# A decoder layer's output product by Strassen's scheme: seven products of half blocks in place of eight

## The chip, the cores and the metric

The kernel runs on one core of one Trainium2 chip. The metric is the device time of one execution in microseconds (us). All times here are of one core. A core has TensorE (PE in the profile; its weight loads have a row of their own, PEld), VectorE (DVE), ScalarE (ACT), GpSimd (POOL) and SyncE (SP, which issues most DMAs). They work at the same time; each takes its own instructions in a fixed order.

## The reference

One layer of a hybrid decoder, on 512 tokens of width 1024, in float32:

```python
h = rms_norm(x, norm_g[l])
proj = h @ w_in[l]
hq, hf, hi, hz, cq, ckv, kr, mz, glog = jnp.split(proj, pts, axis=-1)
y_a = hgrn2_branch(hq, hf, hi, hz, lower_bounds[l], hg_norm_g[l])
y_b = mla_branch(cq, ckv, kr, mz, q_a_g[l], w_uq[l], kv_a_g[l], w_ukv[l])
gates = jax.nn.sigmoid((glog + b_gate[l]).astype(jnp.float32)) ...
merged = gates[:, :, 0] * (y_a @ w_proj_a[l]) + gates[:, :, 1] * (y_b @ w_proj_b[l])
x = x + merged @ w_out[l]
return rms_norm(x, final_norm_g)
```

The change concerns only `merged @ w_out`, a product of 512x1024 with 1024x1024, and what stands right around it: the addition to x and the last RMSNorm.

## The kernel before

Every float32 product is made of three matmuls on a faster format (`mm3`, lines 87 to 92): each operand is split into a high half, rounded to that format, and a low half, the rest; high x high, high x low and low x high are summed in PSUM. The split (`split`, lines 151 to 154) is a copy on ScalarE, which makes the high half, and a subtraction on VectorE, which makes the low half. Weights are loaded by SP's DMAs into a raw tile (pool `wraw`, three buffers) and split into tiles `w_hi` and `w_lo` (pools `whi` and `wlo`, four buffers each; line 111 the copy, 112 the subtraction).

The stage ahead of the change merges the two branches (lines 760 to 791). For each of four groups of 256 channels, and each branch, it makes the gates' logits (a product with the tiles hT, which hold the normed input) and a projection, and combines them. In the second branch VectorE forms (tanh + 1) * projection (line 786), GpSimd adds it into `ma`, the merged activations (line 787), and `split` writes the two halves of `ma` to `m` (line 788). Activations lie with channels on the partitions: `ma[:, j]` holds 128 channels of 512 tokens.

The output stage follows (lines 794 to 842). A block of `w_out` is 128 rows (one k of eight) by all 1024 columns: `load_wo` loads it through `wraw` and splits it into tiles named `wo`. For k from 0 to 3 the weights arrive one by one, and for each k all four blocks of 128 tokens and both halves of the columns are multiplied, into eight PSUM accumulators. Then k from 4 to 7 are finished token block by token block. Behind each half row stand: an addition of half the accumulator to x (line 830, VectorE, out of PSUM; `merged` carries a factor of 2), the sum of squares (833, ScalarE), a product with the norm's gain `fg` (834, VectorE), small operations for the norm on GpSimd (835, 836), the scaling by ScalarE (839) and VectorE (841), and two output DMAs (840 on ScalarE's queue, 842 on SP's).

The program is written with a tile framework: it places waits between instructions that share a tile, and orders the instructions of an engine by a planner, which follows the order of the program as far as its own estimate of readiness allows. Where no `manual_schedule` block stands (none does in the output stage), the order on an engine is the planner's. Pools opened on the same side lie behind each other in memory and take over the memory of closed ones; a tile in such memory waits for the last reader of the tile that lay there. The pool `w_out` on the left thus follows `hpool`, with the tiles hT, whose last readers are the gates' products of the last group of the second branch.

Of the kernel before, what the change touches and what calls it, by code (L numbers as in the profile page):

```python
# [18 lines left out]
P = 128  # L19
D = 1024  # L20
S = 512
NT = S // P
KD = D // P
# [6 lines left out]
EPS = 1e-6  # L30
# [3 lines left out]
N_MM = 3  # L34
WCH = 1024
# [3 lines left out]
def hybrid_layer(ctx: ExitStack, tc: tile.TileContext, a):  # L39
    nc = tc.nc  # L40
# [46 lines left out]
    def mm3(ps, l, r, lsl, rsl, start, stop):  # L87

        (lh, ll), (rh, rl) = l, r
        nc.tensor.matmul(ps, lh[lsl], rh[rsl], start=start, stop=False)  # L90
        nc.tensor.matmul(ps, lh[lsl], rl[rsl], start=False, stop=False)  # L91
        nc.tensor.matmul(ps, ll[lsl], rh[rsl], start=False, stop=stop)  # L92
# [58 lines left out]
    def split(hi, lo, src):  # L151

        last_split[0] = nc.scalar.copy(hi, src)  # L153
        nc.vector.tensor_tensor(lo, src, hi.bitcast(F32), op=ALU.subtract)  # L154
# [17 lines left out]
    neg_half, eps = fixed[:, 0:4], fixed[:, 4:5]  # L172
# [46 lines left out]
    half = [slice(n * 512, n * 512 + 512) for n in range(2)]  # L219
# [54 lines left out]
    with tc.manual_schedule(engines={mybir.EngineType.PE, mybir.EngineType.Activation, mybir.EngineType.DVE}):  # L274
# [17 lines left out]
        sq, rs = st.tile([P, D], F32, "sq", bufs=2), rss[0]  # L292
        v, y, e = [st.tile([P, 1], F32, f"rsq{i}") for i in range(3)]
# [32 lines left out]
        lo = [turned(1, 0), turned(1, 1)]  # L326
        for t in range(1, NT):
# [14 lines left out]
            lo = nxt  # L342
# [5 lines left out]
    ps = ax_tile()  # L348
# [33 lines left out]
    for t in range(NT):  # L382
        ps = mm_tile()
# [22 lines left out]
    for j in range(5):  # L406
        ps = ax_tile()
        for t in range(NT):
# [3 lines left out]
                                       op0=ALU.mult, op1=ALU.subtract)  # L412
    ps = ax_tile()
# [319 lines left out]
    for h in range(H):  # L733
# [12 lines left out]
        if h % 4 == 0:  # L746
            v = mla_values(h)
# [12 lines left out]
    def merge(b, c, y, wp, g=None):  # L760
        return list(zip(g or gates(b, c), proj_ch(wp, c * 256, y)))
# [9 lines left out]
    ma = mp.tile([P, KD, S], F32, "ma")  # L771
# [5 lines left out]
            nc.vector.scalar_tensor_tensor(ma[:, 2 * c + i], g[:], 1.0, ps[:], op0=ALU.add, op1=ALU.mult)  # L777
    yap.close()
    m2p = Pool("merged_parts", "right")
    m = [m2p.tile([P, KD, S], F32R, f"m{i}") for i in range(2)]  # L780
    ybsp = Pool("yb_parts", "right")
    ybs = parts(ybsp, yb, "yb")
    for c in range(4):
        for i, (g, ps) in enumerate(merge(1, c, ybs, a["w_proj_b"][0])):
            j = 2 * c + i
            nc.vector.scalar_tensor_tensor(g[:], g[:], 1.0, ps[:], op0=ALU.add, op1=ALU.mult)  # L786
            nc.gpsimd.tensor_tensor(ma[:, j], ma[:, j], g[:], op=ALU.add)  # L787
# [10 lines left out]
    acc = [mm_tile() for _ in range(N_MM)] + [ax_tile() for _ in range(8 - N_MM)]  # L798
    acc = [acc[2 * t : 2 * t + 2] for t in range(NT)]
    wo = a["w_out"][0].rearrange("(k p) c -> p k c", p=P)  # L800

    def load_wo(k):
        raw = wraw.tile([P, WCH], F32, tag="raw", name="wo_raw")
        hl = [wop.tile([P, 1, D], F32R, f"wo{i}", 4) for i in range(2)]
        nc.sync.dma_start(raw[:], wo[:, k, :])
        split(hl[0][:, 0], hl[1][:, 0], raw[:])
        return hl

    def out_mm(k, t, o, n, w):
        mm3(acc[t][o // 512][:, o % 512 : o % 512 + n], m, w, (slice(None), k, slice(t * P, t * P + P)),  # L810
            (slice(None), 0, slice(o, o + n)), k == 0, k == KD - 1)

    for k in range(4):
        w = load_wo(k)
        for t in range(NT):
            for o in (0, 512):
                out_mm(k, t, o, 512, w)
    ws = [load_wo(k) for k in range(4, KD)]
    nc.sync.dma_start(fg[:], a["final_norm_g"].partition_broadcast(P))
    for t in range(NT):  # L820
        nc.sync.dma_start(xr[t][:], a["x"][0, t * P : t * P + P, :])
    for t in range(NT):
        last = t == NT - 1
        ss = op.tile([P, 3], F32, "ss", bufs=2)
        rg = op.tile([P, D], F32, "rg", bufs=2)
        for i, (o, n) in enumerate(((0, 512), (512, 512))):
            sl = slice(o, o + n)
            for k in range(4, KD):
                out_mm(k, t, o, n, ws[k - 4])
            nc.vector.scalar_tensor_tensor(xr[t][:, sl], acc[t][o // 512][:, o % 512 : o % 512 + n], 0.5, xr[t][:, sl],  # L830
                                           op0=ALU.mult, op1=ALU.add)
            sq = op.tile([P, 512], F32, "sq", bufs=2)
            nc.scalar.activation(sq[:, :n], xr[t][:, sl], AF.Square, accum_out=ss[:, i : i + 1])
            nc.vector.tensor_tensor(rg[:, sl], xr[t][:, sl], fg[:, sl], op=ALU.mult)
            nc.gpsimd.tensor_scalar(ss[:, 0:1], ss[:, i : i + 1], 1.0 / D, ss[:, 0:1] if i else EPS, op0=ALU.mult, op1=ALU.add)
        nc.gpsimd.tensor_tensor(ss[:, 0:1], ss[:, 0:1], neg_half[:, 0:1], op=ALU.pow)
        o = a["out"][0, t * P : t * P + P, :]
        c = 384 if last else 512
        nc.scalar.activation(rg[:, :c], rg[:, :c], AF.Copy, scale=ss[:, 0:1])
        nc.scalar.dma_start(o[:, :c], rg[:, :c])  # L840
        nc.vector.tensor_scalar(rg[:, c:], rg[:, c:], ss[:, 0:1], None, op0=ALU.mult)
        nc.sync.dma_start(o[:, c:], rg[:, c:])
    wop.close()
    op.close()
    m2p.close()
    mp.close()
    edge.close()
# [38 lines left out]
```

## Time and profile before

| | before |
|---|---|
| median of 3 runs | 633.08 us (632.96 to 633.23) |
| the profiled execution's own time | 633.0 us |
| its span, first to last instruction | 631.2 us |
| mean granted TensorE clock | 0.998 |
| busy, ScalarE | 239.6 us (38%) |
| first and last matmul of the output stage start | 580.7 and 624.0 us |

How to read the rows shown in the prediction. On the profile's page, an engine has its busy time, the share of the span, and its number of instructions; the chain that ended last is followed back from the last instruction, and its shares tell which engine's work set the time. A row of a tile gives the line of the kernel, the engine, the operation, output<-inputs, the count, the shortest, median and longest duration in ns, and the first and last start in us. A row of the timeline gives the start, the duration in us, the engine, the line and the operation, with the tile's form, and in brackets how long the engine had been idle and what ended that. A row of the table by stretches gives the busy time of PE, PEld, DVE, ACT and POOL, each with its number of instructions, then the granted clock as a share of full speed, the DMA share, and GB/s. A row of the chain has start, duration, engine and line. A row of DMA issues has the queue, the number, the size of each and the median us from issue to landing.

### The profile page before, as it was taken

Reading aid. Unit: us, or ns where it says so; the run is one execution under the profiler, and the core shown is the slowest. Engines: PE = TensorE matmul, PEld = TensorE weight load, DVE = VectorE, ACT = ScalarE, POOL = GpSimd, SP = SyncE. Lnnn points to the kernel's source line nnn. Section 1 sums busy time; section 2 is a strip of 40 time slices with the busy share of each in tenths; the row PEclk is TensorE's granted clock in tenths of the full one; section 3 lists DMA queues with packets and bytes.
Section 4 is the critical chain, followed back from the end, with each engine's and each line's share of the span. In section 5 each row is a group of like instructions: output and inputs, shape, how many; then the busy total and the mean of one; then the engine's idle time right before and its main releaser. Section 6 shows DMA issues by size and latency. Waiting matters only on the chain.

```text
span 631.2 us, 8391 instructions
## 1 busy us (share of the span) xinstructions
PE 621.8 (99%) x3204; PEld 523.4 (83%) x3204; DVE 353.5 (56%) x552; ACT 239.6 (38%) x451; POOL 115.1 (18%) x213
## 2 busy tenths in 40 slices
PE   8999999999999999999999999999999999999995
PEld 5998888888888888888888888888888888888884
DVE  7727855397855459757566756583322342434244
ACT  5554242323233232355445645382222222323223
POOL 3106300332310033331213141000000010111011
PEclk9999999999999999999999999999999999999999
DMA  8325153124114203322332243213333323325403
GB/s 271 121 63 182 47 167 86 48 67 125 43 38 137 74 21 88 93 62 73 84 96 72 55 130 91 78 37 101 100 101 100 101 73 113 101 82 159 174 16 118
DMA packets 58809, 59.75 MB, mean 95 GB/s; under 512 B 5737, under 2 KB 52239, under 8 KB 58769
## 3 DMA queue, kind: packets, MB, share of 16 engines
q1 hardware_dynamic: 56636, 55.60, 29.5%
q10 hardware_dynamic: 1988, 3.09, 1.7%
q8 instruction: 25, 0.41, 0.3%
q0 software_dynamic: 144, 0.52, 0.3%
q14 instruction: 16, 0.12, 0.1%
HBM read 55.01 MB, written 2.10 MB: 90 GB/s over the span
## 4 chain that ended last, share of the span: by engine, by line
PE 93%; DVE 2%; ACT 2%; POOL 1%; issue 1%; DMA 0%; ACTq 0%; POOLq 0%
PE mm_ps L90 25%; PE mm_ps L92 25%; PE mm_ps L91 25%; PE ax_ps L92 2%; PE ax_ps L91 2%; PE ax_ps L90 2%; PE mm_ps L264 1%; PE ax_ps L664 1%; PE ax_ps L685 1%; PE ax_ps L508 1%; PE ax_ps L229 1%; PE ax_ps L527 1%; PE ax_ps L529 1%; PE ax_ps L496 1%; PE ax_ps L516 1%
## 5 line engine op out<-in xcount | busy, mean ns | idle before, releaser
L112 DVE TENSOR_TENSOR w_lo<-w_raw,w_hi 128x1024 fp32r<-128x1024 f32 (+3 forms) x90 | 109.1, 1216 | 131.5 <-ACT w_hi L111 130.2
L111 ACT CAST w_hi<-w_raw 128x1024 fp32r<-128x1024 f32 (+3 forms) x90 | 89.3, 995 | 179.4 <-PE mm_ps L91 130.0
L90 PE MATMUL mm_ps<-hT,w_hi 128*128 128x512 f32 x384 | 150.8, 393 | 0.0
L91 PE MATMUL mm_ps<-hT,w_hi 128*128 128x512 f32 x384 | 149.8, 390 | 0.0
L92 PE MATMUL mm_ps<-hT,w_lo 128*128 128x512 f32 x384 | 149.6, 391 | 0.0
L92 PEld LDWEIGHTS mm_ps<-hT,w_lo 128*128 128x128 f32 x384 | 72.1, 188 | 14.9
L91 PEld LDWEIGHTS mm_ps<-hT,w_hi 128*128 128x128 f32 x384 | 72.2, 188 | 14.4
L90 PEld LDWEIGHTS mm_ps<-hT,w_hi 128*128 128x128 f32 x384 | 72.2, 188 | 14.2
L787 POOL TENSOR_TENSOR ma<-ma,z 128x512 f32<-128x512 f32 x8 | 11.8, 1479 | 176.9 <-DVE z L786 176.9
L91 PE MATMUL mm_ps<-w_lo,hT 128*128 128x512 f32 (+1 forms) x96 | 36.5, 382 | 0.0
L92 PE MATMUL mm_ps<-w_hi,hT 128*128 128x512 f32 (+1 forms) x96 | 36.4, 382 | 0.0
L90 PE MATMUL mm_ps<-w_hi,hT 128*128 128x512 f32 (+1 forms) x96 | 36.4, 386 | 0.0
L672 POOL TENSOR_SCALAR p<-p,sm 128x128 f32<-128x128 f32 (+3 forms) x28 | 16.9, 606 | 72.9 <-DVE sm L669 59.5
L453 DVE RECIPROCAL tf<-pr 128x512 f32<-128x512 f32 x8 | 26.8, 3349 | 0.2
L670 ACT ACTIVATE p<-ax_ps,sm 128x128 f32<-128x128 f32 (+3 forms) x32 | 16.9, 529 | 25.0 <-DVE sm L669 24.9
L91 PE MATMUL mm_ps<-ya,w_hi 128*128 128x512 f32 x64 | 25.0, 390 | 0.0
L92 PE MATMUL mm_ps<-ya,w_lo 128*128 128x512 f32 x64 | 24.9, 389 | 0.0
L90 PE MATMUL mm_ps<-yb,w_hi 128*128 128x512 f32 x64 | 24.9, 389 | 0.0
L91 PE MATMUL mm_ps<-yb,w_hi 128*128 128x512 f32 x64 | 24.9, 389 | 0.0
L92 PE MATMUL mm_ps<-yb,w_lo 128*128 128x512 f32 x64 | 24.9, 389 | 0.0
L90 PE MATMUL mm_ps<-ya,w_hi 128*128 128x512 f32 x64 | 24.8, 389 | 0.0
L154 DVE TENSOR_TENSOR wo<-wo_raw,wo 128x1024 fp32r<-128x1024 f32 x8 | 9.6, 1223 | 25.9 <-ACT wo L153 25.9
(226 smaller groups left out, 1123.8 us busy)
## 6 DMA issues: line engine op xcount, KB each, us to landing
w_raw<-w_in SPq DMA_DIRECT2D x58, 512.0 KB, 3.8
w_raw<-w_proj_a SPq DMA_DIRECT2D x8, 512.0 KB, 3.4
w_raw<-w_proj_b SPq DMA_DIRECT2D x8, 512.0 KB, 3.4
wo_raw<-w_out SPq DMA_DIRECT2D x8, 512.0 KB, 3.9
xr<-x SPq DMA_DIRECT2D x4, 512.0 KB, 8.9
w_raw<-w_in SPq DMA_DIRECT2D x4, 448.0 KB, 5.0
x<-x SPq DMA_DIRECT2D x3, 512.0 KB, 7.2
w_raw<-w_uq SPq DMA_DIRECT2D x8, 192.0 KB, 2.7
```

The costliest lines, as they stand in the source:

```text
L90: nc.tensor.matmul(ps, lh[lsl], rh[rsl], start=start, stop=False)
L91: nc.tensor.matmul(ps, lh[lsl], rl[rsl], start=False, stop=False)
L92: nc.tensor.matmul(ps, ll[lsl], rh[rsl], start=False, stop=stop)
L111: nc.scalar.copy(hi[:, :o], raw[:, :o])
L112: (lo_eng or nc.vector).tensor_tensor(lo[:, :o], raw[:, :o], hi[:, :o].bitcast(F32), op=ALU.subtract)
L154: nc.vector.tensor_tensor(lo, src, hi.bitcast(F32), op=ALU.subtract)
L229: nc.tensor.matmul(idle[:], zero[:, :P], zero[:], start=True, stop=True)
L264: nc.tensor.matmul(ps, hT[l][:, 4 * kh + k, t * P : t * P + P], c_hl[kh][r][:, k * 256 : k * 256 + 256], start=kh == 0 and kind == 0 and k ...
L453: nc.vector.reciprocal(rp[:], pr[:])
L670: nc.scalar.activation(p[:, :n], sps[:, :n], AF.Exp, scale=SCALE, bias=sm[:, 1:2], accum_out=sm[:, 2:3])
L672: (nc.vector if final else nc.gpsimd).tensor_scalar(p[:, :n], p[:, :n], sm[:, 3:4], 0.5, op0=ALU.mult, op1=ALU.mult)
L787: nc.gpsimd.tensor_tensor(ma[:, j], ma[:, j], g[:], op=ALU.add)
```

## The change

The token-by-k matrix is cut into four blocks: A11 (tokens 0 to 255, channels 0 to 511), A12 (the same tokens, channels 512 to 1023), A21 and A22 (tokens 256 to 511); `w_out` into B11, B12, B21, B22 of 512 x 512. The four blocks of the output are made of seven products of blocks by the scheme of Strassen in Winograd's form, in place of eight. In the order of the code, with the name that the diff gives each operand:

| | product | operand of activations | operand of weights | goes to |
|---|---|---|---|---|
| P1 | A11 B11 | m_top | w11 | u, and output 11 |
| P2 | A12 B21 | m_bot, first tokens | w21 | output 11 |
| P3 | S1 T1 | s1 = A21 + A22 | t1 = B12 - B11 | outputs 22 and 12 |
| P4 | S2 T2 | s2 = S1 - A11 | t2 = B22 - T1 | u, output 12 |
| P5 | A22 T4 | m_bot, last tokens | t4 = B21 - T2 | output 21 |
| P6 | S3 T3 | s3 = A11 - A21 | t3 = B22 - B12 | u, outputs 21 and 22 |
| P7 | S4 B22 | s4 = A12 - S2 | w22 | output 12 |

The sums of blocks are made in place, in float32, on VectorE or GpSimd, and each is then split anew (`a_parts` for activations, `w_parts` for weights). Two blocks of tokens of 128 are made per product, each with 4 k and 3 matmuls of 512 columns. What a product yields is added to x out of PSUM on VectorE (`add_to`), or kept in the running sum `u` (two tiles) which GpSimd adds to x (`add_u`). A21 has no split of its own any more, since no product uses it alone.

All of `w_out` is loaded at once, in eight loads of 512 KB, into tiles of the left pool `w_out`, in place of the three buffers of `wraw`; the split halves are in `whi` and `wlo`, whose four buffers hold two blocks. The loads of x and of the gain are issued behind those of the weights in the program, their tiles lie behind the new pool `sums`.

The core of the diff; `finish` holds the old lines of the norm and the output unchanged but for the order of its small operations:

```diff
-    m = [m2p.tile([P, KD, S], F32R, f"m{i}") for i in range(2)]
+    m_top = [m2p.tile([P, 4, 256], F32R, f"m_top{i}") for i in range(2)]
+    m_bot = [m2p.tile([P, 4, S], F32R, f"m_bot{i}") for i in range(2)]
...
-            split(m[0][:, j], m[1][:, j], ma[:, j])
+            if j < 4:
+                split(m_top[0][:, j], m_top[1][:, j], ma[:, j, 0:256])
+            else:
+                split(m_bot[0][:, j - 4], m_bot[1][:, j - 4], ma[:, j])
...
     wop = Pool("w_out", "left")
+    sp = Pool("sums", "right")
     op = Pool("outp", "right")
...
+    def load_wo(i, j):
+
+        res = []
+        for q in range(2):
+            t = wop.tile([P, WCH], F32, f"wo{i}{j}{q}")
+            k = 4 * i + 2 * q
+            nc.sync.dma_start(t[:].rearrange("p (k c) -> p k c", k=2), wo[:, k : k + 2, 512 * j : 512 * j + 512])
+            res.append(t)
+        return res
+
+    b11, b21, b12, b22 = load_wo(0, 0), load_wo(1, 0), load_wo(0, 1), load_wo(1, 1)
...
+    def w_parts(src):
+        res = []
+        for t in src:
+            hl = [pool.tile([P, WCH], F32R, tag=tag, name=f"wo_{tag}") for pool, tag in ((whi, "hi"), (wlo, "lo"))]
+            split(hl[0][:], hl[1][:], t[:])
+            res.append([v[:].rearrange("p (k c) -> p k c", k=2) for v in hl])
+        return res
+
+    def a_parts(src, nm):
+        t = [sp.tile([P, 4, 256], F32R, f"{nm}{i}") for i in range(2)]
+        split(t[0][:], t[1][:], src)
+        return t
+
+    def minus(eng, out, x, y):
+        eng.tensor_tensor(out, x, y, op=ALU.subtract)
+
+    def product(ap, tok, w, done):
+
+        for t in range(2):
+            ps = ax_tile()
+            for k in range(4):
+                mm3(ps[:], ap, w[k // 2], (slice(None), k, slice(tok + t * P, tok + t * P + P)), (slice(None), k % 2),
+                    k == 0, k == 3)
+            done(t, ps)
+
+    def add_to(t, n, ps):
+
+        sl = xr[t][:, 512 * n : 512 * n + 512]
+        nc.vector.scalar_tensor_tensor(sl, ps[:], 0.5, sl, op0=ALU.mult, op1=ALU.add)
...
+    def squares_half(t, n):
...
+        nc.scalar.activation(sq[:], xr[t][:, sl], AF.Square, accum_out=ss[:, n : n + 1])
+        nc.vector.tensor_tensor(rg[:, sl], xr[t][:, sl], fg[:, sl], op=ALU.mult)
...
+    w11, w21 = w_parts(b11), w_parts(b21)
+
+    u = [z_tile() for _ in range(2)]
+
+    def add_u(t, n, half):
+
+        sl = xr[t][:, 512 * n : 512 * n + 512]
+        nc.gpsimd.tensor_tensor(sl, sl, u[half][:], op=ALU.add)
+
+    def first(t, ps):
+        nc.scalar.activation(u[t][:], ps[:], AF.Copy, scale=0.5)
+        add_u(t, 0, t)
+
+    product(m_top, 0, w11, first)
+    a11, a21, a12, a22 = ma[:, 0:4, 0:256], ma[:, 0:4, 256:512], ma[:, 4:8, 0:256], ma[:, 4:8, 256:512]
+    nc.vector.tensor_tensor(a22, a21, a22, op=ALU.add)
+    s1 = a_parts(a22, "s1")
+    for q in range(2):
+        minus(nc.vector, b11[q][:], b12[q][:], b11[q][:])
+    t1 = w_parts(b11)
+    minus(nc.gpsimd, a21, a11, a21)
+    minus(nc.vector, a11, a22, a11)
+    s2 = a_parts(a11, "s2")
+
+    def row11(t, ps):
+        add_to(t, 0, ps)
+        squares_half(t, 0)
+
+    product(m_bot, 0, w21, row11)
+    b2 = [wraw.tile([P, WCH], F32, tag="raw", name="wo_t2") for _ in range(2)]
+    for q in range(2):
+        minus(nc.gpsimd, b2[q][:], b22[q][:], b11[q][:])
+    t2 = w_parts(b2)
+
+    def both(t, ps):
+        add_to(t + 2, 1, ps)
+        add_to(t, 1, ps)
+
+    product(s1, 0, t1, both)
+    s3 = a_parts(a21, "s3")
+    minus(nc.vector, a12, a12, a11)
+    s4 = a_parts(a12, "s4")
+    for q in range(2):
+        minus(nc.gpsimd, b21[q][:], b21[q][:], b2[q][:])
+    t4 = w_parts(b21)
+
+    def more_u(t, ps):
+        nc.vector.scalar_tensor_tensor(u[t][:], ps[:], 0.5, u[t][:], op0=ALU.mult, op1=ALU.add)
+
+    def second(t, ps):
+        more_u(t, ps)
+        add_u(t, 1, t)
+
+    product(s2, 0, t2, second)
+    for q in range(2):
+        minus(nc.gpsimd, b12[q][:], b22[q][:], b12[q][:])
+    t3 = w_parts(b12)
+    product(m_bot, 256, t4, lambda t, ps: add_to(t + 2, 0, ps))
+    w22 = w_parts(b22)
+
+    def row2(t, ps):
+        more_u(t, ps)
+        for n in range(2):
+            add_u(t + 2, n, t)
+            squares_half(t + 2, n)
+        finish(t + 2, 0, 512)
+
+    product(s3, 0, t3, row2)
+
+    def row12(t, ps):
+        add_to(t, 1, ps)
+        squares_half(t, 1)
+        finish(t, 0, 512 if t == 0 else 384)
+
+    product(s4, 0, w22, row12)
```

More of the change, by code (lines that the diff above doesn't have):

```diff
@@ L797, in hybrid_layer @@
     xr = [op.tile([P, D], F32, "xr", bufs=NT) for _ in range(NT)]
-    acc = [mm_tile() for _ in range(N_MM)] + [ax_tile() for _ in range(8 - N_MM)]
-    acc = [acc[2 * t : 2 * t + 2] for t in range(NT)]
     wo = a["w_out"][0].rearrange("(k p) c -> p k c", p=P)
[L802 to L819, printed above, removed]
+    def load_wo(i, j):
[6 more added lines that the diff above has]
+        return res
@@ L820, in hybrid_layer @@
+    b11, b21, b12, b22 = load_wo(0, 0), load_wo(1, 0), load_wo(0, 1), load_wo(1, 1)
     for t in range(NT):
         nc.sync.dma_start(xr[t][:], a["x"][0, t * P : t * P + P, :])
[L822 to L836, printed above, removed]
+    nc.sync.dma_start(fg[:], a["final_norm_g"].partition_broadcast(P))
@@ L837, in hybrid_layer, with finish @@
+    def finish(t, first, c):
+        ss, rg = sums[t], rgs[t]
+        f, l = ss[:, first : first + 1], ss[:, 1 - first : 2 - first]
+        nc.gpsimd.tensor_scalar(f, f, 1.0 / D, EPS, op0=ALU.mult, op1=ALU.add)
+        nc.gpsimd.tensor_scalar(l, l, 1.0 / D, f, op0=ALU.mult, op1=ALU.add)
+        nc.gpsimd.tensor_tensor(l, l, neg_half[:, 0:1], op=ALU.pow)
         o = a["out"][0, t * P : t * P + P, :]
-        c = 384 if last else 512
-        nc.scalar.activation(rg[:, :c], rg[:, :c], AF.Copy, scale=ss[:, 0:1])
+        nc.scalar.activation(rg[:, :c], rg[:, :c], AF.Copy, scale=l)
```

9 lines of the change are left out of this document (8 added, 1 removed).

## The prediction

> **What bounds the kernel now.** I read the page first: who is busy, and of what the chain that ended last is made.
>
> ```profile
> span 631.2 us, 8391 instructions
> ...
> PE 621.8 (99%) x3204; PEld 523.4 (83%) x3204; DVE 353.5 (56%) x552; ACT 239.6 (38%) x451; POOL 115.1 (18%) x213
> ...
> PE 93%; DVE 2%; ACT 2%; POOL 1%; issue 1%; DMA 0%; ACTq 0%; POOLq 0%
> ```
>
> TensorE is busy in 99% of the span and carries 93% of the chain: the kernel is a row of matmuls without gaps. The other engines matter only where they would open one. Second, the stage of the output product, by stretches of time and by its matmuls:
>
> ```profile
> core 0: us, PE busy (x) PEld busy (x) DVE busy (x) ACT busy (x) POOL busy (x), PEclk, DMA share, GB/s
> 580.00:590.00 10.00, 10.00 (x46) 8.29 (x45) 3.21 (x4) 2.29 (x3) 2.10 (x2) 1.00 0.86 296
> 600.00:610.00 10.00, 10.00 (x46) 8.29 (x45) 1.35 (x2) 1.05 (x1) 0.00 (x0) 1.00 0.01 2
> ```
> ```profile
> L92 PE MATMUL ax_ps<-wo,m x40: 388/389/389, 581.8 to 624.0; 128*128 128x512 f32 x40
> L90 PE MATMUL mm_ps<-wo,m x24: 389/389/389, 580.7 to 609.0; 128*128 128x512 f32 x24
> ...
> L153 ACT CAST wo<-wo_raw x8: 1039/1054/1055, 570.6 to 602.6; 128x1024 fp32r<-128x1024 f32 x8
> L154 DVE TENSOR_TENSOR wo<-wo_raw,wo x8: 1219/1224/1226, 571.6 to 603.7; 128x1024 fp32r<-128x1024 f32 x8
> ```
>
> TensorE stays full and VectorE and GpSimd are nearly idle, so today the stage costs what its matmuls cost. The 192 of them (8 blocks of k, 4 of tokens, 2 of columns, 3 each) start between 580.7 and 624.0: 43.3 over 191 steps is 0.2267 us each; the 389 ns of a row overlap with the next matmul. I call 580.7 T0.
>
> **The change: TensorE.** Seven products of 2 x 4 x 3 = 24 matmuls of the same 512 columns are 168, so 24 fewer: 24 x 0.2267 = 5.44 us saved, and a product (P1 to P7 in the order of the code) lasts 5.44. That is the whole gain on offer, 0.9%.
>
> **The change: VectorE and GpSimd.** What is added are sums of blocks, splits of the sums, and additions behind the products. What one operation costs beside another engine's is seen where the merge stage has both at work: VectorE first, GpSimd behind it.
>
> ```profile
> 516.19 0.69 DVE L154 TENSOR_TENSOR m<-ma,m 128x512 fp32r<-128x512 f32 x1
> 516.79 2.31 DVE L112 TENSOR_TENSOR w_lo<-w_raw,w_hi 128x1024 fp32r<-128x1024 f32 x1
> ...
> 521.88 1.23 DVE L112 TENSOR_TENSOR w_lo<-w_raw,w_hi 128x1024 fp32r<-128x1024 f32 x1 [2.18 <-ACT w_hi L111]
> ```
> ```profile
> 513.63 1.29 POOL L787 TENSOR_TENSOR ma<-ma,z 128x512 f32<-128x512 f32 x1 [119.06 <-DVE z L786]
> 516.35 1.67 POOL L787 TENSOR_TENSOR ma<-ma,z 128x512 f32<-128x512 f32 x1 [1.42 <-DVE z L786]
> ```
>
> GpSimd's addition takes 1.29 us alone. The second one starts at 516.35, while VectorE's subtraction of two SBUF operands runs to 516.88, and ends at 518.02, 1.14 after it. VectorE's next subtraction takes 1.23 alone, but the one from 516.79 ends at 519.10: 1.08 after GpSimd is through. So neither works while the other does; they take turns, and one that has waited then runs some 0.1 shorter. With only one operand from SBUF it is otherwise (VectorE, then GpSimd):
>
> ```profile
> 133.29 1.11 DVE L471 TENSOR_TENSOR k<-ko,gh 128x512 f32<-128x512 f32 x1
> ...
> 134.79 0.67 DVE L549 SCALAR_TENSOR_TENSOR z<-z,mm_ps 128x512 f32<-128x512 f32 x1
> ```
> ```profile
> 133.85 1.50 POOL L450 TENSOR_SCALAR k<-tf,c1n,c 128x512 f32<-128x512 f32 x1
> ```
>
> L471, with two operands from SBUF, delays GpSimd from 133.85 on, whereas L549, whose second operand is in PSUM, runs its 0.67 within GpSimd's 133.85 to 135.35 unhindered. Hence additions out of PSUM (add_to, more_u) are free of the lock, and all sums, all low halves of splits and the products with fg stand in one line with all of GpSimd's additions.
>
> The Trainium skill has two sentences on this. "Advanced Engine Details and Errata", section VectorE Performance Modes, says that GpSimd and VectorE's two-port instructions block each other; read alone it would exempt a plain subtraction of two tensors, which is the first rival below. "SBUF — State Buffer", section Who interferes with whom, counts VectorE instructions with two SBUF inputs against a GpSimd instruction that reads SBUF as well, and has the second one wait for the first to end; the rows above agree with this one.
>
> Now the sum up to P4, whose operands (s2, t2) lie furthest down the line. The first products wait for nothing:
>
> ```profile
> L92 PE MATMUL mm_ps<-hT,w_lo x29: 389/389/389, 539.6 to 569.6; 128*128 128x512 f32 x29
> ```
> ```profile
> wo_raw<-w_out SPq DMA_DIRECT2D x8, 512.0 KB, 3.9
> ```
>
> The new loads of w_out lie in the memory of hT and so start when its last reader ends, at about 570. SP's queue holds only x and fg behind them, which the first additions into xr need at about 584 and which have other memory, so they can go ahead of the loads. At 3.9 us to the first landing and 512 KB per 1.8 us (296 GB/s in the window above), b11 is there at 575.7, b21 at 579.2, b22 at 586.3. Two splits at 1.05 and 1.22 make w11 ready by 578: P1 starts at T0, and P2 behind it.
>
> What VectorE's line still holds at T0 begins with the last merged blocks; the times of those, and of the products with fg, are
>
> ```profile
> 580.86 0.69 DVE L786 SCALAR_TENSOR_TENSOR z<-z,mm_ps 128x512 f32<-128x512 f32 x1 [1.80 <-PE mm_ps L92]
> 581.47 0.69 DVE L154 TENSOR_TENSOR m<-ma,m 128x512 fp32r<-128x512 f32 x1
> 583.98 0.69 DVE L154 TENSOR_TENSOR m<-ma,m 128x512 fp32r<-128x512 f32 x1 [1.83 <-ACT m L153]
> ```
> ```profile
> L834 DVE TENSOR_TENSOR rg<-xr,fg 128x512 f32<-128x512 f32 x8 | 5.4, 688 | 0.2
> ```
>
> VectorE, two operands, T0 to P4, in 1024 columns: the second low half of w21 (its buffer is held by the merge's last weights until T0), two of t1, two of t2, one each of s1 and s2, two sums for b11, one each for a22 and a11: 11 x 1.22 = 13.4. In 512 columns: two splits of m, two products with fg for the first rows: 4 x 0.69 = 2.8. GpSimd: the last addition into ma and two of u into xr, 3 x 1.29 = 3.9; a21 and two for b2 in 1024 columns, for which the trace has no row: between 1.29 (a row of half the width) and 3.3 (twice the blocked 1.67), and I take twice 1.29, 2.58, as VectorE too goes with the width (0.69 to 1.22): 7.7. Also two for b21 and two for b12, which need only early operands. They are not due before P5 and P6, but GpSimd takes what is ready, so I put them in: 10.3. Together 13.4 + 2.8 + 3.9 + 7.7 + 10.3 = 38.1; 25 operations that mostly wait in line, 0.1 less each, make 35.6. So P4 starts at T0 + 35.6 instead of T0 + 16.3: **19.3 us late**. The wait falls about half before P3 (s1 and t1 stand in the same line) and half before P4. Queued behind the waiting operations are ScalarE's high halves and, through them, TensorE.
>
> P4 to P7 have less in the line: nine low halves and sums at 1.22 (s3, s4, t3, t4, w22, a12: 11.0) and two additions of u (2.6), which is 13.6 against the 16.3 from P4's start to P7's, while a split can't begin before the product two earlier gives back its buffers. I allow **1.0**, between 0 and one full turn of 3.8 (2.58 + 1.22).
>
> ScalarE gets 14 high halves of w and 4 of s at 1.05, some 19 us, well below the stage's length, so I charge nothing: its cover is its own idle time, and without it a product waits 1.05.
>
> **The clock.** TensorE would sit idle for some 9 us twice. After its last matmul, and at the start of the kernel, this shows:
>
> ```profile
> 624.40:628.00 3.60, 0.00 (x0) 0.00 (x0) 1.92 (x3) 1.34 (x3) 0.81 (x2) 1.00 0.00 0
> 629.00:631.20 2.20, 0.00 (x0) 0.00 (x0) 0.00 (x0) 0.00 (x0) 0.00 (x0) 0.50 0.32 119
> ```
> ```profile
> 1.18 3.17 PE ax_ps L229 x7
> ...
> 7.10 0.88 PE ax_ps L229 x4
> ```
>
> The granted clock is still 1.00 for 3.6 us of idleness and 0.50 from 4.6 us on. The idle matmuls of the start take 0.45 each from 1.18 on and 0.22 from 7.10 on: up to 5.9 us at half pace, a loss of up to 2.9. The restart before P3 is covered by the line of VectorE; that before P4 is not. Between 0 and 2.9 I take **2.0**. "TensorE: Matmul & The Clock Gate" of the Trainium skill (Part 1: The HAM clock gate) has the full clock return after one busy window of about 3.4 us; by an estimate from that the loss would be 1.7 and the total 0.3 less.
>
> **The end.** Before, it runs from the last matmul to the last output DMA like this:
>
> ```profile
> 624.38 0.70 DVE xr L830
> ...
> 626.00 0.27 POOL ss L835
> 626.30 0.60 POOLq L882
> 626.93 0.62 ACT rg L839
> ```
>
> That is 3.2 us from the last matmul's end to 627.55, and 3.65 more to the span's end. The last row keeps this chain. But the two other token blocks (row2) now have four additions on GpSimd and four products with fg: 4 x 1.29 + 4 x 0.69 = 7.9 in the line. They can start when half of P6 is through and one addition out of PSUM is made (2.7 - 0.8 = 1.9 before P7), and so are done 6.0 after P7's start, later than its 5.44; behind that GpSimd has four times its three small operations (about 1 us each time) and VectorE two more products with fg. **2.5** later, between 0 and 4 (all four finishes behind the last matmul).
>
> Sum: -5.44 + 19.3 + 1.0 + 2.0 + 2.5 = +19.4 on the profiled execution's 633.0, that is 652.4. (The runs before have the median 633.08, 0.08 off.)
>
> **Rivals.** *No line: faster.* If the sums overlapped with GpSimd, P4 would wait for VectorE alone: 13.4 + 2.8 and three more PSUM operations of 0.69 are 18.3 against 16.3, about 1.9 late, and the end would be 0.7 longer: 633.0 - 5.44 + 1.9 + 0.7 = 630.2. For it speaks that VectorE and GpSimd are idle in the windows above; against it speak both blocked pairs. It decides if GpSimd's work costs the path less than 2.8 us (5.44 - 1.9 - 0.7). 0.13.
>
> *GpSimd's early sums held back.* If b21 and b12 stand behind P4's needs, P4 is 9.3 earlier, but P5 then waits for b21 and t4. The bound is the whole line after T0: VectorE 20 x 1.22 + 10 x 0.69 = 31.3 (w11 and half of w21 are done), GpSimd 7 x 2.58 + 9 x 1.29 = 29.7; less 0.1 for each of 46 is 56.4. With no gap at all in it, and 1.5 behind it, it ends at T0 + 57.9, where the kernel before is at T0 + 46.9 (627.55): +11, 644. It is part of the forecast's case, as its lower end.
>
> *Loads late.* If the loads waited for the whole merge stage, until T0, w11 would come 3.9 + 1.8 + 2.3 = 8 us later. All of that falls on the path: 660.4. The last reader of hT at 569.6 speaks against it. 0.07.
>
> **How the numbers follow.** The line decides: 0.80, with 652.4. Range 642 to 665: 2 below the 644 of the packed line, for 1024-wide GpSimd operations faster than 2.58; above, three turns of 3.8 in which the queues' fixed order leaves the line idle, 652.4 + 11.4 = 663.8, which takes in late loads. The two slower cases hold 0.87, of which I leave 0.07 outside, and with them the first rival. A measurement of this kernel can tell about 0.2%, 1.3 us, from no change. Same 0.02: 0.01 from the first rival, its gain eaten up by the end, and 0.01 from the forecast's case. That leaves 0.12 for faster and 0.86 for slower.
>
> **What would show it.** Right: GpSimd rows of about 2.6 us alone and 3.6 to 3.8 in turns, VectorE subtractions of 1.2 that take 3.6 beside them; gaps of TensorE before P3 and P4 that a low half (s1, t1, s2, t2) ends; 168 matmuls of the stage; a clock below 1.00 behind the gaps. Wrong: P2 to P5 without gaps, or 1.2 us rows of VectorE inside GpSimd's; then 630. Gaps ended by a DMA of w_out would be the third rival.

## The result, and the profile after

The changed kernel takes 658.88 us (median of 4 runs, 657.48 to 660.15); the kernel before, in the same runs, 633.02 us. The ratio is 1.0407, 95% interval 1.0379 to 1.0436: slower by 26 us where +19.4 was forecast, and inside the range. The profiled execution took 657.48 us with a span of 655.7, that is 24.5 us over the span before.

The page of the changed kernel, the rows that answer to the first ones of before:

```profile
span 655.7 us, 8398 instructions
...
PE 622.1 (95%) x3180; PEld 521.3 (80%) x3180; DVE 389.6 (59%) x573; ACT 250.7 (38%) x463; POOL 151.6 (23%) x228
...
PE 87%; DVE 8%; DMA 2%; POOL 1%; issue 1%; ACT 1%; SPq 0%; DVEq 0%
```

TensorE executes 24 matmuls fewer, and its busy time is no smaller: behind each wait matmuls run at half pace (rows of 0.63 us instead of 0.39) and count as busy for longer. What tells is the chain, in which 8% is now VectorE, against 2% before. By stretches (us; busy time and instructions of PE, PEld, DVE, ACT, POOL; granted clock; DMA share; GB/s):

```profile
580.00:590.00 10.00, 10.00 (x46) 8.25 (x44) 10.00 (x6) 4.77 (x6) 7.27 (x3) 1.00 0.31 117
590.00:600.00 10.00, 2.79 (x8) 1.17 (x6) 9.96 (x5) 2.13 (x3) 10.00 (x5) 0.71 0.00 0
600.00:610.00 10.00, 7.11 (x20) 5.26 (x21) 9.97 (x6) 2.26 (x5) 10.00 (x5) 0.60 0.00 0
610.00:620.00 10.00, 2.69 (x10) 1.86 (x9) 10.00 (x12) 4.98 (x7) 3.41 (x3) 0.74 0.00 0
```

Before, VectorE was busy for 1.35 us and GpSimd not at all between 600 and 610. Now VectorE is full for 40 us and GpSimd full for 20 of them, and in 590 to 600 the two together are at work on just ten instructions, some of them only in part. The table alone can't say whether both work or one stands still inside its instruction. The timeline of the two engines says it (start, duration, engine, line; a count xN lumps N instructions):

```profile
584.39 8.96 DVE L154 TENSOR_TENSOR wo_lo<-wo,wo_hi 128x1024 fp32r<-128x1024 f32 x3
593.27 2.85 DVE L154 TENSOR_TENSOR m_bot<-ma,m_bot 128x512 fp32r<-128x512 f32 x1
596.15 3.26 DVE L895 TENSOR_TENSOR ma<-ma 128x1024 f32<-128x1024 f32 x1
```
```profile
583.78 2.95 POOL L839 TENSOR_TENSOR wo_t<-wo,wo 128x1024 f32<-128x1024 f32 x1 [2.73 <-DMA wo<-w_out]
586.69 3.37 POOL L839 TENSOR_TENSOR wo<-wo,wo 128x1024 f32<-128x1024 f32 x1
590.02 2.24 POOL L788 TENSOR_TENSOR ma<-ma,z 128x512 f32<-128x512 f32 x1
592.23 3.34 POOL L839 TENSOR_TENSOR wo_t<-wo,wo 128x1024 f32<-128x1024 f32 x1
```

Three low halves of 1024 columns take 2.99 us each on VectorE, where before's took 1.22; 512 columns take 2.85 instead of 0.69. GpSimd's 1.29 has become 2.24. Each row reaches across one of the other engine's: m_bot stands from 593.27 to 596.12, and GpSimd's subtraction ends at 595.57, 0.55 before it. Turns, as forecast. Where TensorE pays for it (its waits in the stage, in brackets the idle time and what ended it):

```profile
592.97 0.50 PE L90 MATMUL ax_ps<-wo_hi,m_bot 128*128 128x512 f32 x1 [2.61 <-ACT m_bot L153]
596.17 1.22 PE L92 MATMUL ax_ps<-wo_hi,m_bot 128*128 128x512 f32 x2 [1.99 <-DVE m_bot L154]
600.54 0.79 PE L90 MATMUL ax_ps<-wo_hi,s 128*128 128x512 f32 x1 [3.15 <-ACT s L153]
604.97 0.79 PE L92 MATMUL ax_ps<-wo_hi,s 128*128 128x512 f32 x1 [2.35 <-DVE s L154]
618.46 0.79 PE L90 MATMUL ax_ps<-wo_hi,s 128*128 128x512 f32 x1 [7.31 <-ACT s L153]
```

P4 begins with the last row, 37.8 us after T0 (580.7) instead of 16.3. The first two rows are waits inside P2 that I had not seen: m_bot's last blocks need GpSimd's last addition into ma (L788 at 590.02), and that stood in GpSimd's queue behind two sums of weights that only P4 and P6 need.

The other long piece is the end. The chain of what ended last, after the last matmul (641.57 to 641.96):

```profile
645.41 0.73 ACT rg L875
646.14 0.02 issue
646.16 2.45 DMA out<-rg
...
648.73 1.30 DVE rg L865 x2
...
650.46 1.30 DVE rg L865 x2
```

Before, the chain of the end held no DMA. Now a product with fg waits for an output DMA: rows 0 and 1 have held both buffers of `rg` since P2, so rows 2 and 3 can begin theirs only when the output of 0 and 1 has left. From the last matmul's end to the end of the span are 13.7 us (641.96 to 655.7), where before had 6.8 (624.37 to 631.2).

### The profile page after: what moved, and what is told of

It reads as the page before. It is cut to its first block, busy times and chain, and to the rows that moved or that the text cites. A ratio compares the mean times of both kernels' runs of the same rounds, so it can differ in the third digit from the quotient of the medians.

```text
span 655.7 us, 8398 instructions
## 1 busy us (share of the span) xinstructions
PE 622.1 (95%) x3180; PEld 521.3 (80%) x3180; DVE 389.6 (59%) x573; ACT 250.7 (38%) x463; POOL 151.6 (23%) x228
## 4 chain that ended last, share of the span: by engine, by line
PE 87%; DVE 8%; DMA 2%; POOL 1%; issue 1%; ACT 1%; SPq 0%; DVEq 0%
PE mm_ps L90 24%; PE mm_ps L92 23%; PE mm_ps L91 23%; DVE wo_lo L154 2%; PE ax_ps L90 2%; PE ax_ps L91 2%; PE ax_ps L92 1%; PE mm_ps L264 1%; PE ax_ps L664 1%; DMA wo<-w_out 1%; PE ax_ps L508 1%; PE ax_ps L685 1%; PE ax_ps L527 1%; PE ax_ps L229 1%; DVE rg L865 1%; PE ax_ps L529 1%
## 5 line engine op out<-in xcount | busy, mean ns | idle before, releaser
L112 DVE TENSOR_TENSOR w_lo<-w_raw,w_hi 128x1024 fp32r<-128x1024 f32 (+3 forms) x90 | 107.1, 1193 | 126.6 <-ACT w_hi L111 125.2
L788 POOL TENSOR_TENSOR ma<-ma,z 128x512 f32<-128x512 f32 x8 | 13.7, 1714 | 175.0 <-DVE z L787 175.0
L154 DVE TENSOR_TENSOR wo_lo<-wo,wo_hi 128x1024 fp32r<-128x1024 f32 x12 | 21.0, 1766 | 15.3 <-ACT wo_hi L153 15.2
```

The lines of the kernel that those rows point to most:

```text
L112: (lo_eng or nc.vector).tensor_tensor(lo[:, :o], raw[:, :o], hi[:, :o].bitcast(F32), op=ALU.subtract)
```

## The experiments

Each ratio is to the kernel before, run together with the edited one. The length of the end is always counted from the last matmul's end in the profiled execution to the end of the span.

**GpSimd's seven sums on VectorE.**

```diff
-    minus(nc.gpsimd, a21, a11, a21)
+    minus(nc.vector, a21, a11, a21)
...
-        minus(nc.gpsimd, b2[q][:], b22[q][:], b11[q][:])
+        minus(nc.vector, b2[q][:], b22[q][:], b11[q][:])
```

(likewise for b21 and b12). Expected:

> The changed kernel, with the seven block sums that GpSimd made now on VectorE; GpSimd keeps only the additions of u and the norm. Theory (one line: a VectorE operation with two SBUF operands and a GpSimd operation take turns): seven operations of about 2.6 us in the line become seven of 1.2, so the line is about 7 x 1.4 = 10 us shorter, of which those before P4 and P5 count: 648 to 652 us, and VectorE's subtractions take 1.2 us again. Rival (VectorE is simply overloaded, GpSimd works beside it): VectorE gets 7 x 1.2 = 8.5 us more in the stretch that TensorE waits for: 663 to 668 us.

Measured: 649.2 us, ratio 1.0254 (1.0239 to 1.0270), 9.7 us less than the changed kernel. Its VectorE:

```profile
591.24 1.21 DVE L839 TENSOR_TENSOR wo_t<-wo,wo 128x1024 f32<-128x1024 f32 x1
592.37 1.21 DVE L839 TENSOR_TENSOR wo<-wo,wo 128x1024 f32<-128x1024 f32 x1
593.51 1.21 DVE L839 TENSOR_TENSOR wo<-wo,wo_t 128x1024 f32<-128x1024 f32 x1
```

With GpSimd quiet, a sum costs 1.21 us. One engine alone does the work of both faster than the two did side by side: GpSimd's sums of weights took some 3 us each and stopped VectorE while they worked. An overload of VectorE, which would have made this kernel slower, is excluded.

**Low halves that read PSUM.** The low halves of the weights are made by subtracting a fixed PSUM tile, in two operations of 512 columns.

```diff
+            nc.vector.tensor_tensor(lo[:, sl], src[:, sl], still[:], op=ALU.subtract)
...
-            split(hl[0][:], hl[1][:], t[:])
+            split_p(hl[0][:], hl[1][:], t[:])
```

> The changed kernel, but the low halves of the seven weight operands are not the difference to the high half: each is made by two VectorE operations that subtract a fixed PSUM tile (so the low halves are not the reference's), 2 x 0.69 = 1.38 us of VectorE in place of 1.22, with one operand from SBUF instead of two. GpSimd's work is unchanged. Theory (turns, and only for two SBUF operands): fourteen operations leave the line, five of them between T0 and P4, so P4 comes some 6 us earlier and the rest of the line is shorter: 649 to 654 us, with these operations at 0.7 us inside GpSimd's. Rival (VectorE overloaded, whatever its operands): VectorE has 14 x 0.16 = 2 us more: 659 to 662 us.

Measured: 653.14 us, ratio 1.032 (1.0304 to 1.0335), 5.7 less, with VectorE given more instructions than before the edit. VectorE, then GpSimd:

```profile
584.47 2.64 DVE L154 TENSOR_TENSOR m_bot<-ma,m_bot 128x512 fp32r<-128x512 f32 x1
587.03 2.47 DVE L833 TENSOR_TENSOR wo_lo<-wo,mm_ps 128x512 fp32r<-128x512 f32 x4
```
```profile
584.16 2.40 POOL L849 TENSOR_TENSOR wo_t<-wo,wo 128x1024 f32<-128x1024 f32 x1 [3.67 <-DMA wo<-w_out]
586.51 2.88 POOL L849 TENSOR_TENSOR wo<-wo,wo 128x1024 f32<-128x1024 f32 x1
```

GpSimd's second subtraction waits until m_bot, with two operands in SBUF, ends at 587.11, and is through 2.28 later, though four operations of VectorE that read PSUM run beside it at 0.6 us each. What makes the turns is the second operand in SBUF.

**Weights loaded earlier.** The blocks of w_out go into the memory of ya and yb, which are dead earlier than hT; the split sums of activations go to hT.

```diff
-            t = wop.tile([P, WCH], F32, f"wo{i}{j}{q}")
+            t = raws[i, j][:, q]
```

> The changed kernel, but w_out is loaded into the memory of ya and yb, free long before, instead of that of hT; the sums of activations go into hT. Theory (the line decides): no product of the changed kernel waits for a load directly; but the line can begin its sums of weights before T0, when b22 lands at 584 now; GpSimd and VectorE both idle some 5 us between 574 and 584, so 3 to 7 us less: 652 to 656 us. Rival (the loads decide): P1 to P4 no longer wait and most of the 26 us goes: below 645 us.

Measured: 644.31 us, ratio 1.0179 (1.0164 to 1.0194). That is 14.6 less, far under what my theory had given, and in the place of the rival by which the loads decide. But GpSimd's timeline allows another reading:

```profile
567.85 2.41 POOL L837 TENSOR_TENSOR wo_t<-yb,ya 128x1024 f32<-128x1024 f32 x1 [6.48 <-ACT z L704]
570.20 2.41 POOL L837 TENSOR_TENSOR yb<-yb 128x1024 f32<-128x1024 f32 x1
575.08 2.40 POOL L837 TENSOR_TENSOR wo_t<-yb,ya 128x1024 f32<-128x1024 f32 x1 [2.47 <-issue]
```

Sums of weights themselves moved ahead of T0, to where VectorE has little to do, and the three shown took 2.4 each. The next experiment tells the two apart.

**The same early loads, the sums held back** behind the last operation of the merge on their engine:

```diff
-        minus(nc.gpsimd, b2[q][:], b22[q][:], b11[q][:])
+        with tc.issue_after(last_ma.ins):
+            minus(nc.gpsimd, b2[q][:], b22[q][:], b11[q][:])
```

> The kernel with early loads, but the sums of weights stand in the queues of VectorE and GpSimd behind the last operation of the merge stage on the same engine (about 583 us), so that the data are early and the sums are not. Theory (the line decides, and the early loads gained because sums could leave it before T0): four sums on GpSimd and two on VectorE, some 4 x 2.4 + 2 x 1.2 = 12 us, come back into the line: 652 to 658 us. Rival (the loads decide): the early data keep their gain, 643 to 647 us.

Measured: 658.26 us, ratio 1.04 (1.0386 to 1.0414), just above the theory's 652 to 658. All of the gain is gone again, with the loads as early as in the experiment before. GpSimd's first sum:

```profile
583.68 3.38 POOL L837 TENSOR_TENSOR wo_t<-yb,ya 128x1024 f32<-128x1024 f32 x1
```

So the loads don't decide; they matter only as far as they let work leave the stretch in which both engines are wanted.

**Does writing take turns too?** Each of GpSimd's seven sums is replaced by two constant fillings of the same tile, which write it whole and read nothing. The kernel so leaves out the sums that P4, P5 and P6 need (three products, not the four of the expectation).

```diff
+        if eng is nc.gpsimd:
+            for _ in range(2):
+                eng.memset(out, 0.5)
```

> The changed kernel, but each of GpSimd's seven block sums is replaced by two fillings of the same tile with a constant (so four of the seven products have wrong operands): GpSimd is about as long busy (2 x 1.0 us each), writes the same tiles, but reads nothing. Theory (turns between two SBUF operands of VectorE and GpSimd's reading): VectorE's subtractions beside the fillings take 1.2 us, and the stage falls to what VectorE alone allows, 634 to 642 us. If writing takes turns as well: VectorE's rows grow to 2.2 us beside them, and some 645 to 652 us remain. Rival (VectorE simply overloaded): no VectorE work is gone, so 655 us and more.

Measured: 640.44 us, ratio 1.0119 (1.0105 to 1.0133), 18.4 less. VectorE, then GpSimd:

```profile
594.76 1.21 DVE L154 TENSOR_TENSOR s<-ma,s 128x1024 fp32r<-128x1024 f32 x1
595.90 1.21 DVE L843 TENSOR_TENSOR ma<-ma 128x1024 f32<-128x1024 f32 x1
```
```profile
594.58 1.97 POOL L841 MEMSET ma<- 128x1024 f32 x2
```

VectorE keeps its 1.21 beside two fillings. GpSimd's turns are taken for reading, not for writing. The fillings also wait for no operand, and how much of the 18.4 us that is worth is not taken apart; the rows show the turns, the total does not measure them alone.

**The end, in four steps.** First, buffers of `rg` of their own for rows 2 and 3, in a dead block of weights:

```diff
-            rgs[t] = op.tile([P, D], F32, "rg", bufs=2)
+            rgs[t] = op.tile([P, D], F32, "rg", bufs=2) if t < 2 else b11[t - 2]
```

> The changed kernel, but the scaled rows rg of the last two token blocks lie in a dead weight tile, so that none of the four shares a buffer with another. Theory (the end is long because two of the four rows wait for the output DMA of the others to give back one of two buffers): in the changed kernel 13.7 us lie between the last matmul and the span's end, 6.8 before; the wait for the DMA (2.5 us) and the two products and scalings strung behind it (some 3 us) go, so about 5 us less, 653 to 655 us. Rival (the end is long because GpSimd's additions and small operations are late): within 1 us of the changed kernel's 658.9.

Measured: 656.55 us, ratio 1.0375 (1.0358 to 1.0393), 2.3 less: short of the theory's 653 to 655, and more than the 1 us of the rival. The wait for the output DMA is gone, and the end still takes 11.5 us (642.3 to 653.8). Next, the four late additions of `u` on VectorE instead of GpSimd:

```diff
-        nc.gpsimd.tensor_tensor(sl, sl, u[half][:], op=ALU.add)
+        (nc.vector if t > 1 else nc.gpsimd).tensor_tensor(sl, sl, u[half][:], op=ALU.add)
```

> The changed kernel (658.9 us) with one edit: the four additions of the half sums to rows 2 and 3, which GpSimd makes in the last stage (5.04 us for the four), are made by VectorE (0.69 us each). It asks what makes up the rest of the long end, 6.9 us above before, of which the two buffers of rg gave back 2.3. Theory: two chains run side by side at the end. Rows 2 and 3 wait for a buffer of rg until the output of rows 0 and 1 has left, and with two buffers that chain alone still ends at about the same place, so the additions alone bring little: 657.0 to 659.5 us. Rival (the additions are the whole rest, the buffers a cost on top of them): 653 to 655.5 us, 4 to 5 us less.

Measured: 657.97 us, ratio 1.0393 (1.0378 to 1.0407), inside the theory's range. But the median hides what the edit did: the end takes 12.0 us (643.5 to 655.5), 1.7 less than the changed kernel's, nearly as much as the buffers gave (2.2), while the last matmul ends 1.5 later. That the additions alone bring little so holds for the total, not for the end, though a wait of 2.62 us for an output DMA still stands in its chain. Then both:

> Both edits of the end in the changed kernel: rows 2 and 3 have buffers of rg of their own in a dead weight tile (alone 656.55 us), and VectorE makes the four late additions instead of GpSimd. Nothing is changed ahead of the last stage. Theory: with both, the end comes back to about that of before, 6.8 us after the last matmul (642.0 in the changed kernel), so 651 to 653.5 us by its median of 658.9. Rival (GpSimd's small operations on the sums of squares, which take turns with VectorE's products, are the rest): 654.5 to 656.5 us.

Measured: 656.79 us, ratio 1.0374 (1.0359 to 1.0388). The theory falls: the end is shorter, 10.4 us (644.9 to 655.3), but not 6.8, and what it gained the stage ahead lost: P4 starts at 620.4 here, at 618.5 in the changed kernel, though nothing ahead of the last stage was edited. In the end that is left, the chain runs through the norm's small operations on GpSimd:

```profile
641.82 1.37 POOL ss L872
643.19 0.07 issue
643.26 0.90 POOL ss L873
644.16 0.03 issue
644.18 0.49 DVE wo L877
```

These two work on one column of 128 values and took 0.27 and 0.55 at the end of before; beside VectorE's products and additions they take 1.37 and 0.90. So they take turns too, and VectorE's scaling, behind which row 0's addition stands, waits for them. Last, the scalings of rows 2 and 3 issued behind the additions and squares of rows 0 and 1:

```diff
-        finish(t + 2, 0, 512)
+        norm(t + 2, 0)
...
-        finish(t, 0, 512 if t == 0 else 384)
+        norm(t, 0)
+        scale(t + 2, 0 if t else D)
+        if t:
+            scale(0, 512)
+            scale(1, 384)
```

> The changed kernel with both edits of the end (656.79 us: its last matmul ends at 644.9, its end takes 10.4 us where the changed kernel's takes 13.7 and before's 6.8) and the scaling of rows 2 and 3 issued behind the additions and squares of rows 0 and 1 in the queues of ScalarE and VectorE. Theory (the end is long because four rows come to their end within two products, and the work of rows 0 and 1 stands in the engines' queues behind scalings of rows 2 and 3 that wait for GpSimd): the end, counted from the last matmul, takes 8.2 to 9.2 us. Rival (GpSimd's norm operations, which take turns with VectorE's, are the whole length): 10 us or more. The median can't tell these apart, since the stage ahead moves by 2.9 us from kernel to kernel (last matmul at 642.0 to 644.9): it should lie between 653 and 657.

Measured: 656.23 us, ratio 1.0367 (1.0353 to 1.0381); the end takes 10.6 us (643.8 to 654.4). The rival had 10 or more, but the run doesn't prove it, since the order that I wanted did not come about. From the chain:

```profile
643.02 0.02 ACT wo L880
643.05 1.03 issue
644.08 0.48 ACT sq L864
```

ScalarE still scales row 2 (L880, for 1.15 us) ahead of row 3's squares: the planner sorted by its own estimate. How the 3.6 us that are left of the end divide between turns and queue order stays open.

**A version after the theory.** Everything of the sums that can be done before T0 is done there, on an idle GpSimd: early loads, T3 = B22 - B12, then T2 = T3 + B11, T4 and S3; the products run in the order P1, P2, P4, P6, P3, P5, P7; a third set of split buffers; `u` is added by VectorE.

```diff
+    for q in range(2):
+        minus(nc.gpsimd, b12[q][:], b22[q][:], b12[q][:])
...
+    for q in range(2):
+        nc.gpsimd.tensor_tensor(b2[q][:], b12[q][:], b11[q][:], op=ALU.add)
+    raw3 = wraw.tile([P, WCH], F32, tag="raw", name="raw_s3")[:].rearrange("p (k c) -> p k c", k=4)
+    minus(nc.gpsimd, raw3, a11, a21)
...
+        minus(nc.vector, b11[q][:], b22[q][:], b2[q][:])
+        minus(nc.gpsimd, b21[q][:], b21[q][:], b2[q][:])
...
-        nc.gpsimd.tensor_tensor(sl, sl, u[half][:], op=ALU.add)
+        nc.vector.tensor_tensor(sl, sl, u[half][:], op=ALU.add)
```

> A version made after the theory, all seven products kept: early loads; the sums of weights and s3 made before T0 (T3 and T2 = T3 + B11 and T4 on GpSimd, T1 = B22 - T2 on VectorE); a third set of two split buffers; the products in the order P1, P2, P4, P6, P3, P5, P7; the additions of u on VectorE; the last scaling of three rows as one VectorE operation; no row waits for another's output DMA. GpSimd has one sum (a12) in the stage. Theory: the line is short enough to hide behind 38.1 us of products, TensorE has no long gaps, the end is as before: 628 to 633 us, against 632.9 before. If VectorE's sheer time (some 39 us in the stage) decides instead: 634 to 638 us.

Measured: 630.24 us (630.17 to 630.48), ratio 0.9957, interval 0.9944 to 0.9971: faster than both kernels. By stretches:

```profile
590.00:600.00 10.00, 10.00 (x46) 8.29 (x45) 10.00 (x11) 4.71 (x7) 1.60 (x2) 1.00 0.00 1
```

(the columns are those of the table above). TensorE has no gap from T0 to its last matmul, which ends at 618.7. VectorE is full here too, but GpSimd has two instructions in ten us. The theory had the end as before; at 9.7 us it gives back 2.9 of the 5.44. In this version too I tried to shorten it, by scaling rows 2 and 3 on ScalarE:

```diff
-        if t != 1:
-            rg = op.tile([P, D], F32, "rg", bufs=2)
-            nc.vector.scalar_tensor_tensor(rg[:], xr[t][:], l, fg[:], op0=ALU.mult, op1=ALU.mult)
-            nc.sync.dma_start(o, rg[:])
+        if t > 1:
+            nc.scalar.activation(rg[:], rg[:], AF.Copy, scale=l)
+            nc.scalar.dma_start(o, rg[:])
```

> The version with the weight sums first (630.24 us, 0.9957 of before) with another end: rows 2 and 3 are multiplied by the final norm's gain early, in halves, and ScalarE scales the whole row, so that no operation of VectorE waits for GpSimd's norm ahead of the additions of rows 0 and 1. In that version the last matmul ended at 618.7 and the end took 9.7 us, where before's took 6.8. Theory (VectorE stood in its queue behind GpSimd): the end takes 6.8 to 7.8 us, 627.4 to 628.5 us. Rival (GpSimd's small operations take turns with VectorE's two-operand products wherever those stand, and the products are now six more): within 0.6 us of 630.2.

Measured: 630.17 us, ratio 0.9956 (0.9944 to 0.9969): no change, as the rival said. The end takes 9.4 us (619.0 to 628.4). The run doesn't prove the rival's cause, since ScalarE now makes two scalings of 1.15 us each ahead of the squares of rows 0 and 1. And with the order of the end as in the last step above:

> The same order of the end in the version with the weight sums first and the rows scaled by ScalarE (630.17 us, its end 9.4 us from the last matmul at 619.0), where the stage ahead has no gap. Theory (queue order): row 1's squares start at 620.6 instead of 621.9 and its scaling ends 1.3 to 1.8 us earlier: 628.3 to 629.0 us. Rival (GpSimd's norm operations in turns with VectorE's): 629.8 to 630.5 us.

Measured: 630.17 us, ratio 0.9955 (0.9942 to 0.9969), end 9.5 us. Again the planner put a scaling (row 3's, on VectorE) ahead of row 1's addition, so here too queue order was not put to the test.

## Why the prediction was right, and where not

**TensorE's work.** 24 matmuls fewer, -5.44: confirmed in the version without gaps, where 168 matmuls start between 580.4 and 618.3, again 0.2267 apart.

**The line up to P4.** Forecast 19.3 us late, measured 21.5 (37.8 less 16.3). The mechanism is shown three ways: without GpSimd's sums (9.7 less), with low halves out of PSUM (5.7 less), and with GpSimd writing alone (18.4 less). This is the term that makes the kernel slower. What the sum missed is about a tenth, although GpSimd's sums were cheaper than I took them (2.40 us alone, not 2.58). I had put the last addition into ma among GpSimd's work, but had not asked what it would be queued behind; P2 waited for it, 4.6 us in two pieces, so that the wait began one product earlier than the forecast's "half before P3, half before P4". That alone did not make P4 later: in the kernel with the sums held back this addition runs at 581.51, ahead of all sums, P2 waits 2.8 us, for VectorE's low halves, and P4 still starts at 619.08.

What P4 lacked longest was the sum for s2, the last of these rows. It overwrites a block that GpSimd's last sum (the one for s3) reads, and that one ended at 612.18:

```profile
611.65 1.61 DVE L154 TENSOR_TENSOR wo_lo<-wo,wo_hi 128x1024 fp32r<-128x1024 f32 x1
613.18 0.68 DVE L853 SCALAR_TENSOR_TENSOR xr<-ax_ps,xr 128x512 f32<-128x512 f32 x1
613.78 0.68 DVE L865 TENSOR_TENSOR rg<-xr,fg 128x512 f32<-128x512 f32 x1
614.38 0.68 DVE L853 SCALAR_TENSOR_TENSOR xr<-ax_ps,xr 128x512 f32<-128x512 f32 x1
614.99 1.21 DVE L154 TENSOR_TENSOR wo_lo<-wo,wo_hi 128x1024 fp32r<-128x1024 f32 x1
616.12 1.21 DVE L839 TENSOR_TENSOR ma<-ma 128x1024 f32<-128x1024 f32 x1
```

The two low halves of weights are, by the order of the program, those of t4, which only P5 needs; I had counted them behind P4's start. The two additions out of PSUM I had called free; free of turns they are, but not of time in VectorE's queue. Behind the last row P4 waits for ScalarE's high half of s2 (1.04 us from 617.36), where my sum has the low half. So the first gaps before P3 and P4 end with a high half, and not with a low one as I had said. How these make up the 2.2 is argued from the rows; no run has one of them alone.

**Clock and waits after P4.** Forecast 2.0 and 1.0, measured 1.6 for both: P4 to P7 are 96 matmuls from 618.46 to 641.57, which is 23.1 us instead of 95 x 0.2267 = 21.5. TensorE has no gap in it; the matmuls start slowly (two of the slow ones, then the first two at full pace):

```profile
619.48 0.63 PE L90 MATMUL ax_ps<-wo_hi,s 128*128 128x512 f32 x1
619.90 0.63 PE L91 MATMUL ax_ps<-wo_lo,s 128*128 128x512 f32 x1
...
621.60 0.40 PE L90 MATMUL ax_ps<-wo_hi,m_bot 128*128 128x512 f32 x1
621.84 0.40 PE L91 MATMUL ax_ps<-wo_lo,m_bot 128*128 128x512 f32 x1
```

They are some 0.43 us apart until 621.6 and 0.23 from there, 3.1 us after the restart at 618.46. These seven steps last 1.55 us longer than at full pace (3.14 less 7 x 0.2267), so nearly all of the 1.6 is the clock. The Trainium skill's page "TensorE: Matmul & The Clock Gate" (Part 1: The HAM clock gate) gives about 3.4 us for the return of the full clock; the trace agrees within the grain of its rows, and the estimate of 1.7 us from it was nearer than my 2.0. Waits for buffers were hidden by the planner, which mixes the matmuls of neighbouring products.

**The end.** This is the step that failed in size: "**2.5** later, between 0 and 4", measured 6.9 (13.7 less 6.8), beyond its upper bound. I had found GpSimd's additions and the products with fg, but not that rows 0 and 1 keep both buffers of `rg` from P2 on, and not that the norm's small operations take turns as well. The buffers alone shorten the end by 2.2, the additions alone by 1.7, both together by 3.3 (13.7 to 10.4); the other 3.6 are left. In the chain of that kernel stand the slowed norm operations and the endings of four rows that follow each other on ScalarE and GpSimd, and how much each has is not taken apart.

Together: -5.44 + 21.5 + 1.6 + 6.9 = +24.5, the difference of the spans. By the forecast the last matmul ends at 624.4 - 5.44 + 19.3 + 1.0 + 2.0 = 641.3, measured 642.0: up to there it was off by 0.7, with errors of 2.2 and -1.4 that nearly cancel, which is luck. Most of what the total missed (24.5 against 19.4) is the end's 4.4.

**The rivals.** *No line* is refuted for this kernel, but its 630.2 is where the version that keeps GpSimd out of the way arrives, by another route: no late P4, and 2.9 for the end instead of the rival's 1.9 and 0.7. *GpSimd's early sums held back*: the opposite happened, GpSimd took them first, ahead of the merge's addition. *Loads late*: the loads of w_out were not what P4 waited for, and loading them earlier, with the sums held where they were, gives 658.26.

## What to carry to other kernels

Before elementwise work is divided between VectorE and GpSimd, look in the trace for pairs of their rows that lie side by side: if a VectorE row is longer there than alone, as here with two operands in SBUF, the engines wait for each other, and the work is better placed on one engine, on PSUM operands, or in a stretch in which the other is idle. A saving of TensorE is worth what the operands' readiness leaves of it: here 5.44 us were on offer, a good order kept 2.7, and the order as written lost 25.9. When a change lets several rows end together, count every buffer and every small operation behind the last matmul, since each of them now has a queue.

## What the runs showed of the hardware that was not expected

- GpSimd's subtraction of two SBUF operands takes 2.40 us alone for 128x1024, a little under twice the 1.29 of its addition of 512 columns; VectorE's takes 1.21.
- GpSimd's fillings don't hold VectorE up at all, and VectorE's operations with one operand in PSUM don't hold up GpSimd. The Trainium skill's "SBUF — State Buffer" (Who interferes with whom) agrees with both: it counts VectorE instructions with two SBUF inputs, and these only against a GpSimd instruction that reads SBUF.
- Even GpSimd's operations on one column wait: 1.37 us instead of 0.27. And the turns are not always one for one. In the kernel with all seven sums on VectorE, one such operation, begun at 602.79, took 8.61 us, while VectorE finished nine operations with two operands in SBUF, one behind the other, at their usual 1.2 and 0.7 us. What lets VectorE keep its turn there, and not beside GpSimd's larger operations, no run shows.

```profile
L871 POOL TENSOR_SCALAR ss<-ss x4: 192/192/8607, 602.8 to 633.5; 128x1 f32<-128x1 f32 x4
```

- Kernels that differ only in the end had their P4 start between 618.5 and 620.4, and the four runs of the changed kernel alone lie 2.7 us apart. That a small shift in which engine is first does this is a guess. The medians of two edits of the end can't be compared more closely than that; the length of the end can, though here it is that of one profiled execution each.
